# Attention stage of an encoder trunk: bulk loads move from SyncE's to GpSimd's DMA queue, and the scores' PSUM banks are laid out first

## The chip, the cores and the metric

The kernel runs on one core of a Trainium2 chip. Its time is in device microseconds (us). The engines that matter here are TensorE (PE), VectorE (DVE), ScalarE (ACT), GpSimd (POOL) and SyncE (SP). SP computes nothing; it issues DMAs, and in the kernel before it issues all of them.

## The reference, cut to what matters

Two groups of tokens (512 and 256, together 768) pass through two layers with shared weights. The change touches the first layer's windowed attention alone:

```python
qkv = h @ w_qkv                                   # h = rms_norm(x), 16 heads of 64, 4 kv heads
logits = einsum('bqgrd,bkgd->bgrqk', qb, kb) * scale + band_bias     # 128-query blocks, keys +-128
m = maximum(max(logits), sink_logit)
pexp = exp(logits - m)
denom = sum(pexp) + exp(sink_logit - m)           # a learned sink per head
probs = pexp / denom
out = einsum('bgrqk,bkgd->bqgrd', probs, vb)
x = x + out @ w_o
```

Behind it follow a squared-ReLU MLP with a gated embedding, then the second layer (a gated convolution in place of attention, and the same MLP and gate), and a last norm.

## The kernel before

**Tiling.** Channels lie on the 128 partitions, the 768 tokens on the free axis. Each float32 product is made of three float32r products (high times high, high times low, low times high); the halves of weights are made on the chip from a raw tile `wraw` (ACT writes `whi`, L657; DVE writes `wlo`, L661). `wraw` has three buffers, the pair `whi`/`wlo` two.

**The attention stage** (`mixer_attention`, L604) takes about the first 262 us of the span. It works group by group (four groups of four heads). `unit(c)` (L1202) fetches `w_q` for heads 2c and 2c+1, makes their product `mm` (L681), scales it into `qt` on DVE (L934, one piece of 512 and one of 256 tokens), splits it into `qh` (ACT) and `ql` (DVE), and then four DMAs from SBUF to SBUF stack high and low half of each head into a tile `q` (L979). Keys go the same way into `kk` (L963). For each of 24 blocks `attend` (L1062) runs: scores `S` on PE (L1087, L1088), reduction on DVE with the bias (L1094), exponential on ACT (L1104), scaling (L1117, L1119), transposes `pt` (L1130), their split `ph`/`pl` (L1139, L1140), products `O` (L1145) and the sum into `heads` (L1161). The sink's column of each logits tile `L` is written by 48 small copies on POOL (L1079), two heads each; `L` has five buffers.

**What sets the order.** In this stage nothing is ordered by program text. Every step is an `Op` with a cost, dependences, and for a DMA the time that its bytes take. `Plan.order` (L538) places them one by one: of the engine that can start first, the ready step with the longest remaining chain. Each engine then runs its steps in that order, and SP's DMAs are issued in that order too. All DMAs share one modelled pipe (L581), and SP may have eight in flight (`LANES`, L481, L572): the built program makes each DMA on SP wait for the landing of the eighth before it. A step of another engine may so change place whenever a cost changes.

**The DMAs of the stage** (L628 `dma`, L639 `fetched`): bulk loads from device memory (`w_q`, `w_k`, `w_v`, `w_o`, `proj`, `p` into `wraw`, and the residual `xa`, L1191); moves of queries and keys; the bias windows, eight DMAs of 96 KB for each group (L1055), read from a skewed table `skew` in device memory; and stores of the embedding's projection `pj`. All of these are on SP.

**PSUM.** The stage's pool gives eight banks by tag: `S` three, `PT` two, `O`, `mm0` and `mm1` one each. A tag gets its banks when the first tile of it is asked for, so in the kernel before `O` has bank 0, `mm0` bank 1, `mm1` bank 2, `PT` 3 and 4, `S` 5 to 7. Behind the stage a new pool of eight banks begins; its first product (L132) writes banks 0 and 1.

Of the kernel before, what the change touches and what calls it, by code (L numbers as in the profile page):

```python
# [10 lines left out]
F32 = mybir.dt.float32  # L11
# [6 lines left out]
P = 128  # L18
D = 1024
KB = D // P  # L20
# [9 lines left out]
BM, BS, BO, BT, BL = 1, 3, 1, 2, 5  # L30
# [20 lines left out]
def trunk_kernel(ctx: ExitStack, tc: tile.TileContext, a: dict, out: bass.AP):  # L51
    nc = tc.nc
    act, dve, pe = nc.scalar, nc.vector, nc.tensor
# [120 lines left out]
    class Norm:  # L174


        n = T
# [299 lines left out]
    class Plan:  # L477


        LATE = 6.0  # L480
        LANES = 8  # L481
        OWN = {"PE": 0.0, "ACT": 0.13, "DVE": 0.12, "POOL": 0.1, "SP": 0.0}
        OTHER = {"PE": 0.22, "ACT": 0.15, "DVE": 0.14, "POOL": 0.3, "SP": 0.1}

# [4 lines left out]
        def op(self, engine, cost, run, after=(), uses=(), behind=(), lands=None):  # L489
            flat = []  # L490
            for d in after:
                flat.extend(d if isinstance(d, (list, tuple)) else [d])
            o = Op(engine, cost, run, [d for d in flat if d is not None], list(behind), lands)
            for key in uses:
                assert key not in self.closed, key
                self.users.setdefault(key, []).append(o)
                if key in self.opened and self.opened[key] not in o.after:
                    o.behind.append(self.opened[key])
            self.ops.append(o)
            o.bonus = self.bonus if engine == "PE" else 0.0  # L500
            return o
# [9 lines left out]
        def first(self, box, engine, cost, run, after=(), uses=(), lands=None):  # L511

            def start():
                box.t = box.make()
                run()

            behind = [box.ahead.op] if box.ahead is not None and box.ahead.op is not None else []
            box.op = self.op(engine, cost, start, [box.free, *after], [box.key, *uses], behind, lands)
            self.opened[box.key] = box.op
            return box.op  # L520
# [17 lines left out]
        def order(self):  # L538
            after = {id(o): 0 for o in self.ops}
            nexts = {id(o): [] for o in self.ops}  # L540
            for o in self.ops:
                for d in o.after + o.behind:
                    nexts[id(d)].append(o)
                after[id(o)] = len(o.after) + len(o.behind)
            known, sorted_ = dict(after), [o for o in self.ops if after[id(o)] == 0]
            for o in sorted_:
                for n in nexts[id(o)]:
                    known[id(n)] -= 1
                    if known[id(n)] == 0:
                        sorted_.append(n)  # L550
            for o in reversed(sorted_):
                tail = o.tail + self.LATE if o.tail is not None else self.OTHER[o.engine]
                o.reach = o.cost + max((n.reach + (tail if o in n.after else 0.0) for n in nexts[id(o)]), default=0.0)
            free = {e: 0.0 for e in self.OWN}
            waiting = {e: [] for e in self.OWN}
            pipe, landings = 0.0, [0.0] * self.LANES

            def offer(o):
                o.ready = max(
                    [self.done(d, o.engine) for d in o.after] + [d.start for d in o.behind], default=0.0  # L560
                )
                waiting[o.engine].append(o)

            for o in self.ops:
                if after[id(o)] == 0:
                    offer(o)
            out = []
            while any(waiting.values()):
                best = None
                for e, os in waiting.items():  # L570
                    if os:
                        t = max(free[e], min(o.ready for o in os), landings[-self.LANES] if e == "SP" else 0.0)  # L572
                        o = max((o for o in os if o.ready <= t), key=lambda o: o.reach + o.bonus)
                        if best is None or t < best[0]:
                            best = t, o
                t, o = best
                waiting[o.engine].remove(o)
                o.start = t
                free[o.engine] = t + o.cost
                if o.tail is not None:  # L580
                    pipe = max(pipe, t + o.cost + 1.3) + o.tail  # L581
                    o.landed = pipe + 0.3
                    landings.append(o.landed)
                o.seq = len(out)
                out.append(o)
                for n in nexts[id(o)]:
                    after[id(n)] -= 1
                    if after[id(n)] == 0:
                        offer(n)
            assert len(out) == len(self.ops)  # L590
            return out
# [12 lines left out]
    def mixer_attention():  # L604
        nonlocal tmp
        s1 = ExitStack()
        psum = s1.enter_context(tc.tile_pool(name="psA", bufs=1, space=PSUM))
        ap = s1.enter_context(tc.tile_pool(name="attn", bufs=2))
        tmp = s1.enter_context(tc.tile_pool(name="tmpA", bufs=3))
        odd = s1.enter_context(tc.tile_pool(name="odd", bufs=2))  # L610

        KHI, KLO, QS = (0, 1, 4, 8), (2, 3, 5, 9), (6, 7, 14, 15, 10, 11, 12, 13)
        PB = {"mm0": 1, "mm1": 1, "S": BS, "O": BO, "PT": BT}
        W0 = SEQS[0]
# [13 lines left out]
        def dma(box, src, n, after=(), uses=(), queue="SP", rate=400e3):  # L628

            def run():  # L630
                d, s = src()
                (nc.sync if queue == "SP" else act).dma_start(d, s)

            lands = n / rate
            if box is not None and box.op is None:
                return first(box, queue, 0.46, run, after, uses, lands)
            return op(queue, 0.46, run, after, uses, lands=lands)

        def fetched(src):  # L639
            n = src.shape[1]  # L640
            raw = new("wraw", 3, lambda: wp.tile([P, CH], F32, name="wraw", bufs=3))
            raw.n = n
            raw.landed = [dma(raw, lambda: (raw.t[:, :n], src), P * 4 * n, uses=())]
            return raw

        def pair_tiles():
# [54 lines left out]
        def halves(w, xs, tags, col=0, fine=False):  # L701

            o, out = 0, []
            for tag, n in zip(tags, SEQS):
                ps = bank(tag)
                out.append((ps, o, n, product(ps, w, xs, o, n, col, fine)))
                o += n
            return out
# [479 lines left out]
        def load_part(ms):  # L1188
            for m in ms:
                xa[m] = place(m, "xa", F32)  # L1190
                xa[m].ready = [dma(xa[m], lambda m=m: (xa[m].t[:], a["x"][m]), 393216)]  # L1191

        def output_part(m, w, n, col=0):
            ops = []
# [5 lines left out]
                op("DVE", V(e), run, [last, xa[m].ready], [ps.key, xa[m].key])  # L1200

        def unit(c, tag):  # L1202
            queries(c, prepared(fetched(a["w_q"][c]), KB), ("mm0", "mm1"), tag)

        def second_keys():
            keys(1, halves(prepared(fetched(a["w_k"][1]), KB), xs, ("mm0", "mm1")), "t")

        def second_projected():
            ps = [pair(2 + p, "p1", F32R) for p in range(2)]
            part1 = []  # L1210
            for k in range(2):
                raw = fetched(a["p"][1, :, k, :])

                def high(k=k, raw=raw):
                    act.activation(ps[0].t[:, k, :], raw.t[:, :T], AF.Copy)

                def low(k=k, raw=raw):
                    dve.tensor_tensor(ps[1].t[:, k, :], raw.t[:, :T], ps[0].t[:, k, :].bitcast(F32), ALU.subtract)

                if k == 0:  # L1220
                    h = first(ps[0], "ACT", A(T), high, [raw.landed], [raw.key])
                    l = first(ps[1], "DVE", V(T), low, [h], [raw.key, ps[0].key])
                else:
                    h = op("ACT", A(T), high, [raw.landed, h], [raw.key, ps[0].key])
                    l = op("DVE", V(T), low, [h, l], [raw.key, ps[0].key, ps[1].key])
                b = Box()
                b.parts = lambda k=k: [p.t[:, k, :] for p in ps]
                b.ready, b.keys = [h, l], [p.key for p in ps]
                part1.append(b)
            w = prepared(fetched(a["proj"][1, 0]), 2)  # L1230
            for m in range(KB // 2):
                projected(1, m, w, part1, temp("n", "pjs"), ("mm0",), False)

# [16 lines left out]
        load_part(range(4))  # L1250
        group_of_heads(2)
        for j in range(2):
            w = prepared(fetched(a["w_o0"][j]), 4)
            for i in range(2):
                output_part(2 * j + i, w, 4, i * P)
        split_heads(2)
        load_part(range(4, KB))
        group_of_heads(3)
        for m in range(4, KB):
            output_part(m, prepared(fetched(a["w_o1"][m - 4]), 6), 6)  # L1260
        split_heads(3)
        with s1:
            with tc.manual_schedule(engines={ET.Activation, ET.PE, ET.DVE, ET.SP, ET.Pool}):
# [1193 lines left out]
```

## Time and profile before

| | us |
|---|---|
| median of three runs | 1643.17 |
| lowest, highest | 1642.59, 1643.72 |
| the profiled execution's own time | 1643.69 |
| span of its trace | 1641.9 |
| outside the span | 1.8 |

The page of the whole run reads: PE 1625.1 us busy (99% of the span), PE weight loads 1573.5 (96%), DVE 1389.6 (85%), ACT 920.6 (56%), POOL 12.3 (1%). The granted TensorE clock is at its full value in all 40 slices of the span. A busy PE in these views includes the overlap of pipelined matmuls, so a better measure of lost PE time is the idle time that the timeline puts in square brackets ahead of an instruction, with the event that ended it. The chain of work that ended last is 92% PE, 4% DVE and 2% DMA.

### The profile page before, as it was taken

How to read it: one execution, taken by the hardware profiler on the slowest of the kernel's cores; microseconds unless marked ns; L12 is line 12 of the kernel's file. 1: busy time of each engine (PE TensorE's matmuls, PEld its weight loads, DVE VectorE, ACT ScalarE, POOL GpSimd, SP SyncE). 2: the span in 40 equal slices, each digit the busy share in tenths (PEclk: the TensorE clock that was granted, in tenths of full speed). 3: DMA queues.
4: the chain of work that ended last, by engine and by line, in shares of the span. 5: the costliest groups of instructions: out<-in, count | busy, mean ns of one | idle time of the engine just before them, and what ended most of it. 6: DMA issues, size and time to landing. Idle time of an engine off the chain costs nothing.

```text
span 1641.9 us, 24136 instructions
## 1 busy us (share of the span) xinstructions
PE 1625.1 (99%) x9371; PEld 1573.5 (96%) x9371; DVE 1389.6 (85%) x2212; ACT 920.6 (56%) x1458; POOL 12.3 (1%) x60
## 2 busy tenths in 40 slices
PE   9999999999999999999999999999999999999998
PEld 7888889999999999999999999999999999999987
DVE  7578888999899989977878888768989989998686
ACT  7478885755555545545654344555555555654455
POOL 0000000000000000000000000000000000000000
PEclk9999999999999999999999999999999999999999
DMA  8745302212122212122311222211122121211322
GB/s 307 196 131 141 102 27 97 103 65 78 65 77 70 72 66 88 66 96 75 116 61 53 77 78 77 78 52 63 67 74 81 64 76 68 76 71 71 119 95 88
DMA packets 47822, 144.80 MB, mean 88 GB/s; under 512 B 6075, under 2 KB 9531, under 8 KB 47708
## 3 DMA queue, kind: packets, MB, share of 16 engines
q1 hardware_dynamic: 47708, 143.27, 25.7%
q8 instruction: 73, 1.20, 0.3%
q14 instruction: 41, 0.34, 0.1%
HBM read 123.85 MB, written 9.96 MB: 81 GB/s over the span
## 4 chain that ended last, share of the span: by engine, by line
PE 92%; DVE 4%; DMA 2%; ACT 1%; issue 1%; SPq 0%; DVEq 0%; ACTq 0%
PE a L465 33%; PE b L465 8%; PE mm L681 7%; PE mm L132 6%; PE p L1494 6%; PE d L465 5%; PE c L465 5%; PE gate L1828 4%; PE B L465 4%; PE C L465 4%; PE gate L132 3%; PE down L1828 2%; PE pt L1130 1%; PE O L1145 1%; PE S L1087 1%; PE S L1088 1%
## 5 line engine op out<-in xcount | busy, mean ns | idle before, releaser
L433 ACT ACTIVATE whi<-sum 128x1024 fp32r<-128x1024 f32 x66 | 70.2, 1063 | 253.6 <-PE a L465 251.8
L465 PE MATMUL a<-xs,whi 128*128 128x384 f32 x608 | 117.7, 334 | 0.0
L465 PEld LDWEIGHTS a<-xs,whi 128*128 128x128 f32 x608 | 106.4, 188 | 0.4 <-DVE t L2233 0.4
L465 PE MATMUL a<-t,zhi 128*128 128x384 f32 x528 | 106.6, 334 | 0.0
L465 PE MATMUL a<-t,whi 128*128 128x384 f32 x528 | 106.6, 334 | 0.0
L465 PE MATMUL b<-t,zhi 128*128 128x384 f32 x528 | 106.6, 334 | 0.0
L1650 DVE TENSOR_TENSOR x<-x,a 128x384 f32<-128x384 f32 x112 | 62.1, 554 | 51.5 <-PE a L465 51.5
L465 PE MATMUL a<-act,whi 128*128 128x384 f32 x448 | 95.6, 334 | 0.0
L465 PEld LDWEIGHTS a<-t,whi 128*128 128x128 f32 x528 | 92.9, 188 | 0.0
L465 PEld LDWEIGHTS b<-t,zhi 128*128 128x128 f32 x528 | 92.9, 188 | 0.0
L465 PEld LDWEIGHTS a<-t,zhi 128*128 128x128 f32 x528 | 92.9, 188 | 0.0
L433 ACT ACTIVATE zhi<-sum 128x1024 fp32r<-128x1024 f32 x66 | 69.8, 1057 | 40.8 <-DVE sum L409 26.1
L444 DVE TENSOR_TENSOR wlo<-wraw,whi 128x1024 fp32r<-128x1024 f32 x72 | 87.7, 1218 | 0.0
L433 ACT ACTIVATE whi<-wraw 128x1024 fp32r<-128x1024 f32 x72 | 75.7, 1052 | 20.1 <-issue 15.6
L444 DVE TENSOR_TENSOR zlo<-sum,zhi 128x1024 fp32r<-128x1024 f32 x66 | 80.4, 1218 | 0.7 <-ACT zhi L433 0.7
L681 PE MATMUL mm<-xs_mix,whi 128*128 128x512 f32 (+1 forms) x320 | 80.8, 339 | 0.0
L444 DVE TENSOR_TENSOR wlo<-sum,whi 128x1024 fp32r<-128x1024 f32 x66 | 80.4, 1219 | 0.0
L465 PEld LDWEIGHTS a<-act,whi 128*128 128x128 f32 x448 | 79.3, 188 | 0.0
L465 PE MATMUL a<-xs,wlo 128*128 128x384 f32 x304 | 64.9, 334 | 0.0
L465 PE MATMUL a<-t,wlo 128*128 128x384 f32 x264 | 60.9, 334 | 0.0
L465 PE MATMUL a<-t,zlo 128*128 128x384 f32 x264 | 60.9, 334 | 0.0
L465 PE MATMUL b<-t,zlo 128*128 128x384 f32 x264 | 60.9, 334 | 0.0
(391 smaller groups left out, 4477.3 us busy)
## 6 DMA issues: line engine op xcount, KB each, us to landing
wraw<-in_up SPq DMA_DIRECT2D x64, 512.0 KB, 3.4
wraw<-in_down SPq DMA_DIRECT2D x64, 512.0 KB, 3.4
wraw<-in_w_in SPq DMA_DIRECT2D x24, 512.0 KB, 3.5
wraw<-in_gate SPq DMA_DIRECT2D x16, 512.0 KB, 3.5
wraw<-in_w_q SPq DMA_DIRECT2D x8, 512.0 KB, 7.1
wraw<-in_w_out SPq DMA_DIRECT2D x8, 512.0 KB, 3.5
x_in<-in_x SPq DMA_DIRECT2D x8, 384.0 KB, 7.3
pj<-L SPq DMA_DIRECT2D x8, 384.0 KB, 5.7
```

Of the source, the lines that this page charges most:

```text
L132: pe.matmul(t, lhsT=w, rhs=x[:, o:e], start=first and i == 0 and j == 0, stop=last and i == n - 1 and j == 2)
L433: act.activation(hi[:], src, AF.Copy)
L444: dve.tensor_tensor(lo[:], src, hi[:].bitcast(F32), ALU.subtract)
L465: pe.matmul(ps, lhsT=a, rhs=b, start=start and i == 0, stop=i == len(terms) - 1, skip_group_check=True)
L681: pe.matmul(ps.t[:, :n], lhsT=a_, rhs=b_, start=k == 0 and j == 0, stop=k == len(xs) - 1 and j == 2,)
L1087: pe.matmul(S.t[:, :w], lhsT=q, rhs=khh_[g].t[:, kk], start=True, stop=False)
L1088: pe.matmul(S.t[:, :w], lhsT=q, rhs=kll_[g].t[:, kk], start=False, stop=True)
L1130: pe.transpose(pt.t[:, h * P : (h + 1) * P], lg[h // 2].t[:, h % 2, 1 + b * P : 1 + (b + 1) * P], ident[:],)
L1145: pe.matmul(O.t[:], lhsT=vb, rhs=part.t[:], start=b == 0 and i == 0, stop=b == nk - 1 and i == 1)
L1494: pe.matmul(ps[i][o], lhsT=wt[:, c], rhs=xs[f"x{h + 1}{1 + o}"][m][part], start=k == 0 and j == 0, stop=k == KB - 1 and j == 2,)
L1650: dve.tensor_tensor(t[:, o : o + H], t[:, o : o + H], f, op)
L1828: pe.matmul(ps.t[:, o : o + n], lhsT=a_, rhs=b_, start=begin and i == 0 and j == 0, stop=end and i == len(terms) - 1 and j == 2,)
```

## The change

It has three parts.

1. The bulk loads of the stage behind its first ones (`w_q` from the third on, the second `w_k`, the second layer's `p` and `proj`, all `w_o`, and the eight `xa`) are issued on POOL's queue. The start of the kernel (`proj`, `p`, `x`, `w_k`, two `w_q`, `w_v`) stays on SP, as do moves of queries and keys, the bias and the stores: of 367 DMA rows in SP's program 24 go to POOL's.
2. The planner counts 1.0 us of POOL for such an issue (0.46 on SP), has a pipe and a list of landings for each queue instead of one for all, and adds 1.0 us to a landing on POOL's. Its order of the whole stage is made anew with these numbers.
3. Ahead of everything else a tile of each of the tags `S`, `PT` and `O` is asked for, so `S` gets banks 0 to 2, `PT` 3 and 4, `O` 5, `mm0` 6 and `mm1` 7.

```diff
+        EXTRA = {"POOL": 1.0}
...
-            pipe, landings = 0.0, [0.0] * self.LANES
+            pipe, landings = {}, {e: [0.0] * self.LANES for e in self.OWN}
...
-                        t = max(free[e], min(o.ready for o in os), landings[-self.LANES] if e == "SP" else 0.0)
+                        t = max(free[e], min(o.ready for o in os), landings[e][-self.LANES] if e == "SP" else 0.0)
...
-                    pipe = max(pipe, t + o.cost + 1.3) + o.tail
-                    o.landed = pipe + 0.3
-                    landings.append(o.landed)
+                    pipe[o.engine] = max(pipe.get(o.engine, 0.0), t + o.cost + 1.3) + o.tail
+                    o.landed = pipe[o.engine] + 0.3 + self.EXTRA.get(o.engine, 0.0)
+                    landings[o.engine].append(o.landed)
...
+        for tag in ("S", "PT", "O"):
+            psum.tile([P, 512], F32, tag=tag, name="unused", bufs={"S": BS, "PT": BT, "O": BO}[tag])
...
-                (nc.sync if queue == "SP" else act).dma_start(d, s)
+                {"SP": nc.sync, "POOL": nc.gpsimd, "ACT": act}[queue].dma_start(d, s)
...
-        def fetched(src):
+        def fetched(src, queue="SP"):
...
-            raw.landed = [dma(raw, lambda: (raw.t[:, :n], src), P * 4 * n, uses=())]
+            raw.landed = [dma(raw, lambda: (raw.t[:, :n], src), P * 4 * n, queue=queue)]
...
-                xa[m].ready = [dma(xa[m], lambda m=m: (xa[m].t[:], a["x"][m]), 393216)]
+                xa[m].ready = [dma(xa[m], lambda m=m: (xa[m].t[:], a["x"][m]), 393216, queue="POOL")]
...
-            queries(c, prepared(fetched(a["w_q"][c]), KB), ("mm0", "mm1"), tag)
+            queries(c, prepared(fetched(a["w_q"][c], "POOL"), KB), ("mm0", "mm1"), tag)
...
-            w = prepared(fetched(a["w_o0"][j]), 4)
+            w = prepared(fetched(a["w_o0"][j], "POOL"), 4)
...
-            output_part(m, prepared(fetched(a["w_o1"][m - 4]), 6), 6)
+            output_part(m, prepared(fetched(a["w_o1"][m - 4], "POOL"), 6), 6)
```

Three places show what the new order does. The first is SP's queue in the middle of the stage, where the third and fourth groups' queries (`q`), the second keys and the bias are moved. Before:

```order
L632 DMA wraw<-in_w_o 128x1024
L632 DMA kk<-qh 64x768 x4
L632 DMA kk<-ql 64x768 x4
L632 DMA q<-qh 64x768 x2
L632 DMA wraw<-in_w_o 128x1024
L632 DMA q<-ql 64x768 x2
L632 DMA xa<-in_x 128x768 x2
L632 DMA bias<-skew 32x2x384 x8
L632 DMA q<-qh 64x768 x2
L632 DMA wraw<-in_w_o 128x768
L632 DMA q<-ql 64x768 x2
```

and now:

```order
L635 DMA kk<-qh 64x768 x4
L635 DMA kk<-ql 64x768 x4
L635 DMA q<-qh 64x768 x2
L635 DMA q<-ql 64x768 x2
L635 DMA bias<-skew 32x2x384 x8
L635 DMA q<-qh 64x768 x2
L635 DMA q<-ql 64x768 x2
```

The two loads of `w_o` that stood between a query's high and low halves, and the two of `xa` ahead of the bias, are gone from the queue; the eight bias DMAs still stand ahead of the next queries.

The second place is POOL's queue over the same stretch and a little beyond, where before only the sink copies stood (48 in a row):

```order
L1083 COPY L<-nsink 128x2 x10
L635 DMA wraw<-in_w_o 128x1024
L635 DMA xa<-in_x 128x768 x2
L1083 COPY L<-nsink 128x2 x4
L635 DMA wraw<-in_w_o 128x768
L1083 COPY L<-nsink 128x2 x4
L635 DMA wraw<-in_w_o 128x768
```

The loads now stand among the copies, which go on in the order of the blocks that need them.

The third place is PE, between the projection of heads 10 and 11 (`mm`, for the query tile that is read at the end) and the first scores that read that tile (`q_2004` before, `q_2007` now). The last rows before:

```order
L681 MATMUL mm_1939<-xs_mix0_372,wlo_1812 128x512
L681 MATMUL mm_2053<-xs_mix0_181,whi_1811 128x256
L681 MATMUL mm_2053<-xs_mix0_193,whi_1811 128x256
L681 MATMUL mm_2053<-xs_mix0_181,wlo_1812 128x256
L681 MATMUL mm_2053<-xs_mix0_230,whi_1811 128x256
L681 MATMUL mm_2053<-xs_mix0_257,whi_1811 128x256
L681 MATMUL mm_2053<-xs_mix0_230,wlo_1812 128x256
L681 MATMUL mm_2053<-xs_mix0_261,whi_1811 128x256
L681 MATMUL mm_2053<-xs_mix0_282,whi_1811 128x256
L681 MATMUL mm_2053<-xs_mix0_261,wlo_1812 128x256
L1087 MATMUL S_2066<-kk_1538,q_2004 128x256
```

and now:

```order
L1149 MATMUL O_2041<-pl_2043,vv_105 128x512
L685 MATMUL mm_1942<-xs_mix0_375,whi_1814 128x512
L685 MATMUL mm_1942<-xs_mix0_407,whi_1814 128x512
L685 MATMUL mm_1942<-xs_mix0_375,wlo_1815 128x512
L1091 MATMUL S_2056<-kk_1541,q_2007 128x256
```

The nine matmuls on 256 tokens have gone from ahead of the scores. Otherwise the same 36 matmuls stand between the last one of that projection and these scores: 21 `mm` on 512 tokens, 2 `S` on 256, 5 `O` and 8 transposes.

More of the change, by code (lines that the diff above doesn't have):

```diff
@@ L631, in run @@
                 d, s = src()
-                (nc.sync if queue == "SP" else act).dma_start(d, s)
+                {"SP": nc.sync, "POOL": nc.gpsimd, "ACT": act}[queue].dma_start(d, s)
             lands = n / rate
+            cost = 1.0 if queue == "POOL" else 0.46
             if box is not None and box.op is None:
-                return first(box, queue, 0.46, run, after, uses, lands)
-            return op(queue, 0.46, run, after, uses, lands=lands)
-        def fetched(src):
+                return first(box, queue, cost, run, after, uses, lands)
+            return op(queue, cost, run, after, uses, lands=lands)
+        def fetched(src, queue="SP"):
             n = src.shape[1]
@@ L1202, in unit @@
         def unit(c, tag):
-            queries(c, prepared(fetched(a["w_q"][c]), KB), ("mm0", "mm1"), tag)
+            queries(c, prepared(fetched(a["w_q"][c], "POOL"), KB), ("mm0", "mm1"), tag)
         def second_keys():
-            keys(1, halves(prepared(fetched(a["w_k"][1]), KB), xs, ("mm0", "mm1")), "t")
+            keys(1, halves(prepared(fetched(a["w_k"][1], "POOL"), KB), xs, ("mm0", "mm1")), "t")
         def second_projected():
@@ L1211, in second_projected @@
             for k in range(2):
-                raw = fetched(a["p"][1, :, k, :])
+                raw = fetched(a["p"][1, :, k, :], "POOL")
                 def high(k=k, raw=raw):
@@ L1229, in second_projected @@
                 part1.append(b)
-            w = prepared(fetched(a["proj"][1, 0]), 2)
+            w = prepared(fetched(a["proj"][1, 0], "POOL"), 2)
             for m in range(KB // 2):
```

## The prediction, made before the change was run

> **What bounds the kernel now.** I read the page first, then the windows, then the waits, and last the timelines at the places that the waits name. The page's chain of work that ended last:
>
> ```profile
> PE 92%; DVE 4%; DMA 2%; ACT 1%; issue 1%; SPq 0%; DVEq 0%; ACTq 0%
> ```
>
> PE sets the end nearly everywhere, so only a stretch in which PE waits can give time back. The windows (busy us of PE, PEld, DVE, ACT, POOL; clock; DMA share; GB/s) show where such stretches lie:
>
> ```profile
> 100.00:125.00 25.00, 24.84 (x152) 21.27 (x151) 24.01 (x73) 24.76 (x65) 1.85 (x10) 1.00 0.58 181
> 150.00:175.00 25.00, 20.94 (x122) 17.90 (x121) 18.03 (x52) 15.26 (x41) 2.24 (x6) 1.00 0.59 141
> 300.00:325.00 25.00, 25.00 (x147) 25.00 (x146) 21.76 (x32) 16.50 (x22) 0.00 (x0) 1.00 0.15 55
> ```
>
> Behind the attention stage PE is full (300 to 325 us). Inside it most windows are nearly full too; the one from 150 to 175 us lacks 4 us, on PE, DVE and ACT alike, so all three wait there for something else. The waits over 100 to 250 us name it, and PE's timeline shows each place (start, length, what ran; in brackets the idle time before it and what ended it):
>
> ```profile
> PE S L1087 <- DMA q<-ql: 4.8, 3, 2.7
> ```
>
> ```profile
> 155.35 0.35 PE L1087 MATMUL S<-kk,q 128*128 128x256 f32 x1 [1.34 <-DMA q<-ql]
> ...
> 167.53 0.36 PE L1087 MATMUL S<-kk,q 128*128 128x256 f32 x1 [2.71 <-DMA q<-ql]
> ...
> 207.04 0.39 PE L1087 MATMUL S<-kk,q 128*128 128x256 f32 x1 [0.75 <-DMA q<-ql]
> ...
> 262.33 0.94 PE L132 MATMUL mm<-aos,whi 128*128 128x384 f32 x4 [0.60 <-DVE xa L1198]
> ```
>
> Three times scores wait for the low half of their queries, 4.8 us in all; and the first product behind the stage waits 0.60 us until DVE has emptied a bank. That is all that this change can win by removing waits. SP's queue tells why the queries are late:
>
> ```profile
> 146.61 1.10 SPq L632 DMA_DIRECT2D q<-qh  x2
> 147.81 0.53 SPq L632 DMA_DIRECT2D wraw<-in_w_o  x1
> 148.44 1.10 SPq L632 DMA_DIRECT2D q<-ql  x2
> 149.63 1.09 SPq L632 DMA_DIRECT2D xa<-in_x  x2
> 150.82 8.95 SPq L632 DMA_DIRECT2D bias<-skew  x8
> 159.87 1.11 SPq L632 DMA_DIRECT2D q<-qh  x2
> 161.07 0.54 SPq L632 DMA_DIRECT2D wraw<-in_w_o  x1
> 161.71 1.10 SPq L632 DMA_DIRECT2D q<-ql  x2
> ```
>
> A load of `w_o` stands between the halves each time, and the eight bias issues take 8.95 us, because SP waits for the landing of the eighth DMA before: of the waits of SP's queue from 146 to 162 us,
>
> ```profile
> SPq L632 <- DMA xa<-in_x: 2.8, 2, 1.7
> SPq L632 <- DMA wraw<-in_w_o: 1.9, 1, 1.9
> ```
>
> What a query's move costs without and with a load ahead of it, from issue to landing (median us), is in the DMA view of 92 to 98.5 us, where nothing else is in flight, and of 140 to 165 us:
>
> ```profile
> q<-ql SPq DMA_DIRECT2D x4, 192.0 KB, 4.0
> ```
>
> ```profile
> q<-ql SPq DMA_DIRECT2D x4, 192.0 KB, 6.2
> ```
>
> **The change part by part.** *The first wait (1.34 us).* PE's rows up to these scores (`q_1840`) are the same in number and kind before and now. DVE and ACT made this query's halves here, and the next one's 12 us later:
>
> ```profile
> 147.02 0.95 DVE L716 TENSOR_TENSOR ql<-qt,qh 128x768 fp32r<-128x768 f32 x1
> ...
> 156.45 0.42 DVE L934 SCALAR_TENSOR_TENSOR qt<-mm,rstd_mix 128x256 f32<-128x256 f32 x1
> ...
> 158.90 0.95 DVE L716 TENSOR_TENSOR ql<-qt,qh 128x768 fp32r<-128x768 f32 x1
> ```
>
> The low half is ready at 147.97; issued at once and landing in 4.0 us, it is there at 152.0, and PE came to the scores at 155.35 - 1.34 = 154.0. I take the whole 1.34; the other end is 0, if `w_o` on its own queue slows the move as much as one ahead of it does.
>
> *The second wait (2.71 us).* PE's work between the projection and these scores shrinks by nine matmuls on 256 tokens. Their price, and that of the 36 that stay, from the chain in order of time:
>
> ```profile
> 174.11 0.36 PE mm L681 x3
> ...
> 175.59 0.68 PE mm L681 x3
> 176.26 0.23 PE O L1145
> 176.50 0.87 PE pt L1130 x8
> ```
>
> Three matmuls on 256 tokens take 0.36, so 0.12 each; three on 512 take 0.68, 0.23 each; eight transposes 0.87. The nine are 1.1 us, which are not lost but run later. What stays is 21 x 0.23 + 2 x 0.12 + 5 x 0.23 + 0.87 = 7.1 us. The projection is done when its last `qt` starts, 156.45, so PE reaches the scores at 163.5. The low half is ready at 158.90 + 0.95 = 159.85; before, it was issued at 161.71. With `w_o` and `xa` off SP neither of the two waits of SP above stands ahead of it, and at 159.9 + 4.0 it lands at 163.9. I leave 0.5 us of waiting and take 2.2 saved; the ends are 0 and 2.71.
>
> *The third wait (0.75 us).* `w_o` is gone from between the halves, and counted with the same prices PE has 9.2 us of work ahead of the first scores of heads 14 and 15 instead of 8.0. All 0.75 are taken (ends 0 and 0.75).
>
> *The bank (0.60 us).* Banks 0 and 1, which L132 writes first, are now two of the scores' banks, last read several us earlier, and no longer `O` and `mm0`. `mm0` and `mm1` (now 6 and 7) are asked for only two products later. I take 0.60; the ends are 0 and 0.60.
>
> *What it costs.* Sooner scores in the first group: there PE's work between the projection of heads 2 and 3 and their first scores falls from 8.9 to 7.5 us (12 value products on 256 tokens no longer stand there). In exchange a load of `p` is gone from between the high halves on SP:
>
> ```profile
> 67.05 0.53 SPq L632 DMA_DIRECT2D wraw<-in_p  x1
> ```
>
> That load's issue of 0.53 and its share of the DMA engines go, 1.4 of cover go; I put 0.3 for it, between 0 and 1.4. Then POOL: no load is issued there before, so its price is bounded by the nearest rows: 0.53 (SP's issue) from below; from above, two sink copies that took 1.50, 1.13 more than the 0.37 of the row shown next:
>
> ```profile
> 158.40 1.50 POOL L1079 COPY L<-nsink 128x2 f32<-128x2 f32 x2 [6.32 <-PE pt L1130]
> ```
>
> so 0.5 to 1.7 us an issue. Queued behind a load are the sink copies, for which DVE's reduction waits. Nine of the 24 loads come ahead of the sixth copy, fifteen stand among the others. What hides them is that a copy is made when its `L` comes free, mostly some us ahead of the reduction; early it is not so:
>
> ```profile
> 97.64 0.37 POOL L1079 COPY L<-nsink 128x2 f32<-128x2 f32 x2 [57.50 <-PE pt L1130]
> ```
>
> ```profile
> 97.84 0.61 DVE L1094 CUSTOM_DVE_ANT_0 L<-S,bias,nsink 128x384 f32<-128x384 f32 x1
> ```
>
> At 97.84 the reduction follows the first copy at once. I put 0.5 us for one such late copy, nearest to the lower row; the ends are 0 and 17 (15 x 1.13). That the loads themselves land later costs nothing at first: before, ACT waited 0.3 us in all for a `w_q`,
>
> ```profile
> ACT whi L657 <- DMA wraw<-in_w_q: 0.3, 1, 0.3
> ```
>
> as each is fetched while earlier products run; without that cover each later landing would hold ACT's queue.
>
> *The sum:* 1.34 + 2.2 + 0.75 + 0.60 = 4.9 won, 0.3 + 0.5 lost, 4.1 in all. From the profiled execution's 1643.69 that leaves 1639.6. That execution lies 0.52 above the median of the runs, so the forecast is **1639.1**.
>
> **The rivals.** *Same bytes, same engines.* The loads are only put in another queue, and share the DMA engines with the queries at the same moments (their share is 0.59 over 150 to 175 us). If a move beside `w_o` takes the 6.2 us that it took behind it, the three waits stay, and only the bank's 0.60 is won, with 0.8 of costs: 1643.4. For it speaks that the load still starts about when the query's halves are ready; against it that FIFO order put all 512 KB ahead of 192 KB, and that sharing puts at most as much. The Trainium skill has this as a rule ("DMA: Bandwidth & Descriptors", section "Issuing engines are not separate DMA queues"): DMAs of all issuing engines run on the same 16 DMA engines and interleave, and a second issuer saves only the time of issuing. By that rule this rival is the case; the trace so far shows order within one queue, none between two.
>
> *POOL's queue holds DVE* (the slower side). A load on POOL waits in order for its buffer and then takes POOL; the copies behind it come late, the reductions on DVE with them, and DVE has no room (24.01 of 25 us busy from 100 to 125). With half of 15 x 1.13 on the path, 8.5 us in place of my 0.5, it ends at 1647.1. It eats the gain when each of the fifteen costs the path 0.31 us (4.6 / 15), and makes the kernel slower by 0.2% from 0.53 on. For it speaks the row with 1.50; against it, the row at 97.64, whose copies took 0.37 beside a DVE at work. The skill ("SBUF — State Buffer", section "SBUF: two separate sides") names a cause that would bring it about: GpSimd cannot write a DMA's descriptors while certain VectorE instructions hold a port that both share. No run here has yet shown such a DMA.
>
> That the planner's new order loses PE time elsewhere is part of both; PE's rows are the same kinds in the same number.
>
> **How the numbers follow.** Forecast 0.52, same bytes 0.25, POOL's queue 0.23. A measurement of this kernel can tell about 0.2%, 3.3 us, from no change: faster means below 1639.9, slower above 1646.5. The forecast's own range is 1637 to 1641, of which about three quarters lie below 1639.9 (0.40) and the rest within 0.2% (0.12); the second case lies within (0.24, and 0.01 above); the third is slower (0.23). The range goes from 1637 (both costs nothing, and all 2.71 saved: 1637.8, with a little for a better order elsewhere) to 1648, into the third case.
>
> **What would show it.** In the profile after, the waits of `S` L1087 for `q<-ql` should fall from 4.8 us to under 1, the eight bias issues from 8.95 us to about 4, `q<-ql` to near 4.0 us to landing, and L132 should start with no wait for `xa`. Waits of `L` L1094 for POOL, or of `whi` L657 for DMAs of POOL's queue, would speak for the slower rival; waits for `q<-ql` as before for the other. The forecast is wrong if PE's loss over 100 to 262 us does not shrink.

## The result: 0.58% slower, and the profile after

| | before | after |
|---|---|---|
| median, us | 1643.83 (6 runs) | 1653.71 (6 runs) |
| lowest, highest | 1642.59, 1644.41 | 1649.83, 1655.70 |
| profiled execution: own time, span | 1643.69, 1641.9 | 1655.32, 1653.5 |
| start of the first product behind the attention stage (L132) | 262.33 | 273.13 |
| from there to the end of the span | 1379.6 | 1380.4 |

The ratio of the times is 1.0058, 95% interval 1.0047 to 1.0069. The last two rows say where to look: 10.8 of the 11.6 us that the span grew lie inside the attention stage. Lines of that stage have moved down by four in the new kernel (scores L1091, values L1018, reduction L1098, `xa` L1202, the split of `p` L1219 and L1222).

Three views of the profile after. The first is the chain of work that ended last; DMA had 2% of it before:

```profile
PE 88%; DVE 5%; DMA 4%; ACT 1%; issue 1%; SPq 0%; DVEq 0%; POOL 0%; ACTq 0%; POOLq 0%
```

The second is PE's timeline at the places of the stage from 50 us on where it stood still for half a microsecond or more (start, length; in brackets the idle time and what ended it):

```profile
55.92 0.48 PE L1018 MATMUL vp<-wvh,xs_mix 128*128 128x256 f32 x1 [3.29 <-DVE vv L1036]
...
80.24 0.55 PE L1091 MATMUL S<-kk,q 128*128 128x256 f32 x1 [3.07 <-DMA q<-ql]
...
164.73 0.36 PE L1091 MATMUL S<-kk,q 128*128 128x256 f32 x1 [1.34 <-DMA q<-ql]
...
175.05 0.36 PE L1091 MATMUL S<-kk,q 128*128 128x256 f32 x1 [1.92 <-DMA q<-ql]
...
214.47 0.35 PE L1091 MATMUL S<-kk,q 128*128 128x256 f32 x1 [1.77 <-DMA q<-ql]
...
273.13 0.94 PE L132 MATMUL mm<-aos,whi 128*128 128x384 f32 x4 [0.60 <-DVE xa L1202]
```

The first two are new. The first wait of before (1.34) and the bank's 0.60 are unchanged to the hundredth, 2.71 became 1.92, and 0.75 became 1.77. The third view is windows of 4 us around the two new gaps and the one at 175 us (busy PE, PEld, DVE, ACT, POOL; granted clock; DMA share; GB/s):

```profile
52.00:56.00 4.00, 0.71 (x4) 0.27 (x2) 1.35 (x2) 1.21 (x2) 0.12 (x1) 1.00 1.04 223
56.00:60.00 4.00, 4.00 (x18) 3.71 (x19) 0.00 (x0) 0.00 (x0) 0.42 (x1) 0.57 1.06 230
...
80.00:84.00 4.00, 3.76 (x14) 3.38 (x15) 1.74 (x5) 1.21 (x4) 0.00 (x0) 0.58 0.39 131
...
176.00:180.00 4.00, 4.00 (x18) 3.71 (x17) 2.25 (x8) 1.91 (x6) 0.00 (x0) 0.63 0.02 6
```

Behind each of these gaps PE worked for some 3.5 us at a granted clock of about half. Worked out as busy time times the missing clock, that cost 1.7, 1.6 and 1.5 us more. Before, the granted clock was 1.00 in the windows behind its longest gap, 2.71 us.

So the account of the stage is: 5.0 us at 52 us (3.29 and the clock), 4.7 at 77, 0.7 at 173 (1.92 and 1.5 against 2.71), and 1.0 at 212. That is 11.4, against 10.8 by which the stage became longer.

**How the gap at 52 us comes about** is told by ACT's timeline, before and after:

```profile
50.76 0.48 ACT L1029 ACTIVATE vv<-vp,rc 128x256 fp32r<-128x256 f32 x1 [4.24 <-PE vp L1016]
61.35 0.84 ACT L1215 ACTIVATE p<-wraw 128x768 fp32r<-128x768 f32 x1 [10.12 <-DMA wraw<-in_p]
```

```profile
53.64 0.84 ACT L1219 ACTIVATE p<-wraw 128x768 fp32r<-128x768 f32 x1 [7.29 <-DMA wraw<-in_p]
54.39 0.46 ACT L1033 ACTIVATE vv<-vp,rc 128x256 fp32r<-128x256 f32 x1
```

Before, ACT waited longer for the second layer's `p` (10.12 us), but the value copy `vv` stood ahead of it, so nothing was held up by that. Now the same split of `p` stands ahead of `vv`; the in-order engine holds `vv` until the load has landed, and PE's next value product waits for the bank that `vv` and DVE's half of it must empty. The DMA view of 43 to 51 us has the load and its neighbours (KB each, median us from issue to landing):

```profile
kk<-qh SPq DMA_DIRECT2D x4, 192.0 KB, 9.0
...
wraw<-in_p POOLq DMA_DIRECT2D x1, 384.0 KB, 7.9
```

The planner's own sum for that load on a POOL pipe that is free is 1.0 (issue) + 1.3 + 393216/400000 + 0.3 + 1.0 = 4.6 us. It took 7.9, beside moves of keys that the plan has on another pipe with a full rate of its own. At 77 us it is the same with a move: on SP's free pipe the plan's sum for two moves behind each other is 0.46 + 1.3 + 2 x 196608/215000 + 0.3 = 3.9 us, and in the DMA view of 72 to 79 us

```profile
wraw<-in_proj POOLq DMA_DIRECT2D x1, 512.0 KB, 6.8
...
q<-ql SPq DMA_DIRECT2D x2, 192.0 KB, 6.8
```

### The profile page after: what moved, and what is told of

Its sections match the earlier page's. It is cut to its first block, busy times and chain, and to the rows that moved or that the text cites. A ratio compares the mean times of both kernels' runs of the same rounds, so it can differ in the third digit from the quotient of the medians.

```text
span 1653.5 us, 24160 instructions
## 1 busy us (share of the span) xinstructions
PE 1629.2 (99%) x9371; PEld 1576.8 (95%) x9371; DVE 1390.1 (84%) x2212; ACT 920.6 (56%) x1458; POOL 24.4 (1%) x84
## 4 chain that ended last, share of the span: by engine, by line
PE 88%; DVE 5%; DMA 4%; ACT 1%; issue 1%; SPq 0%; DVEq 0%; POOL 0%; ACTq 0%; POOLq 0%
PE a L465 33%; PE b L465 8%; PE mm L132 6%; PE p L1498 6%; PE mm L685 6%; PE d L465 5%; PE c L465 5%; PE B L465 4%; PE C L465 4%; PE gate L1832 3%; PE gate L132 2%; PE down L1832 2%; DMA q<-ql 1%; PE pt L1134 1%; PE O L1149 1%
```

## The experiments

Two theories were set against each other. *Order:* the loss comes from the new order of steps on in-order engines, planned with landings that are too early, since each queue has a pipe of its own. *Queue:* loads on POOL's queue cost by themselves.

### 1. The queue alone (e1), the order alone (e2), the banks alone (e3), one pipe (e4)

e1 keeps the planner and banks of before (`cost` is 0.46 for all), so PE, ACT and DVE have the order of before, row for row (the edit against the kernel before, cut):

```diff
+                {"SP": nc.sync, "POOL": nc.gpsimd, "ACT": act}[queue].dma_start(d, s)
...
+            return op("SP" if queue == "POOL" else queue, cost, run, after, uses, lands=lands)
```

> The 24 bulk loads are issued on POOL's queue, but the planner still counts them on SP with one common pipe, so PE, ACT and DVE run their steps in the order of the kernel before; the banks are as before. Order theory (the loss comes from the steps' new order, which rests on landings that the planner puts too early because each queue has a pipe of its own): 1641 to 1645 us, the two new PE stalls at 52 and 77 us (3.3 and 3.2 us) are gone. Queue theory (loads on POOL's queue cost by themselves, through shared DMA engines, POOL's time or later landings): at least 6 of the 10 us stay, 1649 to 1655.

Measured: 1645.84 us, ratio 1.0013 (1.0004 to 1.0022), 0.8 us beyond the range of the order theory; the stage ends at 265.1 us. Both new gaps are gone, and most of the loss with them, but not all of it. Two other waits for queries nearly cancel (a new one of 0.76 us at 74 us, and the second wait down from 2.71 to 0.98). What is left of the loss lies at the third wait, 0.75 us before, and in 1.6 us of low clock behind it; on PE's timeline:

```profile
208.56 0.36 PE L1089 MATMUL S<-kk,q 128*128 128x256 f32 x1 [3.10 <-DMA q<-ql]
```

The DMA views of 198 to 209 us, of before and of e1, tell why:

```profile
q<-qh SPq DMA_DIRECT2D x2, 192.0 KB, 2.9
wraw<-in_w_o SPq DMA_DIRECT2D x1, 384.0 KB
q<-ql SPq DMA_DIRECT2D x2, 192.0 KB, 5.2
```

```profile
xa<-in_x POOLq DMA_DIRECT2D x1, 384.0 KB, 5.5
q<-qh SPq DMA_DIRECT2D x2, 192.0 KB, 6.6
q<-ql SPq DMA_DIRECT2D x2, 192.0 KB, 7.8
wraw<-in_w_o POOLq DMA_DIRECT2D x1, 384.0 KB, 7.5
```

In one queue the high halves were issued ahead of `w_o` and landed in 2.9 us, as if it were not there. From two queues everything in flight shares the DMA engines, and all of it lands late: 6.6 us for the high halves, 7.8 instead of 5.2 for the low ones, and 5.5 for the last load of `xa`, where the last two took 3.5 before (DMA view of 197 to 198 us). Sharing does not explain all of it: the low halves were issued 1.1 us sooner than before (200.62 against 201.74), with about the same bytes moved (2.0 MB in either view), and still landed 1.5 us later. The rest stays open. The Trainium skill has the rule ("DMA: Bandwidth & Descriptors", section "Issuing engines are not separate DMA queues"): DMAs of all issuing engines run on the same 16 engines and interleave. The runs agree: a second queue is no second set of engines. They add that a move can lose by it.

e2 is the reverse: order and banks of the changed kernel, all loads on SP.

```diff
-                {"SP": nc.sync, "POOL": nc.gpsimd, "ACT": act}[queue].dma_start(d, s)
+                {"SP": nc.sync, "POOL": nc.sync, "ACT": act}[queue].dma_start(d, s)
```

> The changed kernel's order and banks, but its 24 bulk loads are issued on SP's queue at the place that the order gives them. Order theory: the value copy on ACT still stands behind the split of the second layer's in_p, so the PE stall at 52 us stays at 2 us or more and the time is 1649 to 1658 us. Queue theory: near the kernel before, 1642 to 1646.

Measured: 1657.69 us, ratio 1.0088 (1.0074 to 1.0102), slower than the change as a whole. PE stands for 4.62 us at 52 us, and loses the clock again:

```profile
57.42 0.50 PE L1018 MATMUL vp<-wvh,xs_mix 128*128 128x256 f32 x1 [4.62 <-DVE vv L1036]
```

The order brings the loss without POOL's queue. In this order the second queue even helps.

e3 adds only the two lines of the banks to the kernel before.

```diff
+        for tag in ("S", "PT", "O"):
+            psum.tile([P, 512], F32, tag=tag, name="unused", bufs={"S": BS, "PT": BT, "O": BO}[tag])
```

> The kernel before with the scores' banks first in the pool; every engine's order as before. If the bank that L132 waits for was the one that the output's sum still read, 0.60 us of idle time at 262 us go and the time is 1642.6. If the wait is for the whole pool, or for another bank that the same sum reads, the 0.60 us stay, and the time is that of the kernel before within 0.5 us. The order theory needs the second; no theory has this part cost anything.

Measured: 1643.35 us, ratio 1.0001 (0.9992 to 1.0009), and in PE's timeline

```profile
261.36 0.94 PE L132 MATMUL mm<-aos,whi 128*128 128x384 f32 x4 [0.60 <-DVE xa L1200]
```

The products write banks 0 and 1, which are now the scores', and still wait for the last sum on DVE, which reads another bank. It isn't for data either, since the product reads `aos` and `whi` and not `xa`. So the wait isn't that of the bank. That it hangs on the whole pool being given back is likely, but was not tried.

e4 is the changed kernel with one pipe in the planner.

```diff
-            pipe, landings = {}, {e: [0.0] * self.LANES for e in self.OWN}
+            pipe, landings = 0.0, {e: [0.0] * self.LANES for e in self.OWN}
...
+                    pipe = max(pipe, t + o.cost + 1.3) + o.tail
+                    o.landed = pipe + 0.3 + self.EXTRA.get(o.engine, 0.0)
```

> The changed kernel, but the planner has one common pipe for all DMAs again; its issue cost of 1.0 us on POOL, its added landing of 1.0 us and the banks stay. Its order is then almost that of the kernel before on PE. Order theory: 1641 to 1646 us, no stall of 3 us at 52 or 77. Queue theory: 1649 to 1655.

Measured: 1647.31 us, ratio 1.0023 (1.0014 to 1.0032): 1.3 us beyond what the order theory gave, far from what the queue theory gave. The pipe alone so accounts for 6.4 of the 9.9 us by which the changed kernel was slower. The gap at 52 us is gone; four waits for queries are left, two of 1.4 us at 159 and 170 and two longer ones, each with the low clock behind it:

```profile
75.34 0.36 PE L1091 MATMUL S<-kk,q 128*128 128x256 f32 x1 [2.21 <-DMA q<-ql]
...
211.54 0.36 PE L1091 MATMUL S<-kk,q 128*128 128x256 f32 x1 [2.65 <-DMA q<-ql]
```

### 2. Later landings in the plan (e5 to e7)

If the plan's landings are too early, adding to them must help, with the queues as they are. e5:

```diff
-        EXTRA = {"POOL": 1.0}
+        EXTRA = {"POOL": 6.0}
```

> The changed kernel, but the planner adds 6 us instead of 1 to a landing on POOL's queue. PE's order stays that of the changed kernel between projections and scores; on ACT the split of the second layer's in_p falls from ahead of the second value copy to behind it. Order theory: only the stall at 52 us goes, 3.4 us, and with it the 1.7 us in which the granted clock was 0.66 behind it: 1647 to 1650 us, the stalls at 77, 163, 173 and 212 us stay. If the low clock has another cause than the idle time, it stays and the time is 1650 to 1651. Queue theory: 1652 or more, since no load moves to another queue.

Measured: 1649.43 us, ratio 1.0038 (1.0025 to 1.0050). The gap at 52 us is gone, and the clock behind it is whole; of the two windows, the second is the one that had 0.57 in the changed kernel:

```profile
52.00:56.00 4.00, 4.00 (x26) 3.48 (x25) 0.48 (x1) 0.48 (x1) 0.00 (x0) 1.00 1.02 205
56.00:60.00 4.00, 4.00 (x28) 3.66 (x27) 0.96 (x1) 0.85 (x1) 0.54 (x1) 1.00 1.06 222
```

The stage became 3.6 us shorter than the changed kernel's, not 5.0, because the wait of 1.92 us grew to 3.03, with twice as long a low clock behind it:

```profile
170.55 0.55 PE L1091 MATMUL S<-kk,q 128*128 128x256 f32 x1 [3.03 <-DMA q<-ql]
```

e6 corrects both queues by about what the traces show:

```diff
-        EXTRA = {"POOL": 1.0}
+        EXTRA = {"POOL": 4.0, "SP": 3.0}
```

> The changed kernel, but the planner adds 4 us to a landing on POOL's queue and 3 us to one on SP's, so that it plans with about the 6 to 8 us that loads and moves took beside each other. PE's work between a projection and its first scores grows from 7.5 to 10.2 us for heads 2 and 3, from 7.1 to 10.1 for heads 10 and 11, and from 9.2 to 10.9 for the last. Order theory: the stalls at 52, 77, 173 and 212 us shrink to under 1 us each, and the time is 1640 to 1645. Queue theory: 1649 or more. A third possibility is that the later scores leave DVE and ACT idle and PE loses as much elsewhere: 1646 to 1650.

Measured: 1638.75 us, ratio 0.9970 (0.9958 to 0.9981): faster than both kernels, 15 us below the changed one, and 1.2 us below what the order theory gave. Two waits for queries are left on PE's timeline:

```profile
155.76 0.36 PE L1091 MATMUL S<-kk,q 128*128 128x256 f32 x1 [1.15 <-DMA q<-ql]
...
166.72 0.35 PE L1091 MATMUL S<-kk,q 128*128 128x256 f32 x1 [0.59 <-DMA q<-ql]
```

e7 has the order of e6 with all loads issued on SP (the edit of e2 on top of that of e6).

> The order of the kernel that counts both queues' landings 3 to 4 us later, but all its loads are issued on SP's queue, in that order. It tells what the queue is worth once the order leaves time for the landings. Order theory: the queue is worth little by then, within 2 us of the same order with POOL's queue. If two queues really help (as with the changed kernel's own order, which was 4 us slower on SP alone): 3 to 6 us slower. If POOL's queue costs by itself: faster.

Measured: 1640.02 us, ratio 0.9975 (0.9964 to 0.9985). The intervals of e6 and e7 overlap widely. Once the order leaves room for the landings, the queue is worth nothing that can be told here.

### 3. The kernel before with later landings (e8, e9, e11), and two queues on one pipe (e10)

With that, the change isn't needed for the gain. e8, e9 and e11 are the kernel before, all DMAs on SP, with 1.5, 3 and 6 us added to every landing in the plan; for e8:

```diff
-                    o.landed = pipe + 0.3
+                    o.landed = pipe + 1.8
```

> The kernel before, all DMAs on SP and one common pipe, but its planner adds 1.5 us to every landing. PE's work ahead of the first scores grows from 8.2 to 9.4 us for heads 10 and 11 and from 8.0 to 11.2 for the last, with ql ahead of w_o at heads 10 and 11. Order theory: the waits for queries (4.8 us before) fall to 1 to 2 us, and the kernel beats both, 1639 to 1642. If the later scores cost DVE and ACT as much: 1642 to 1646.

Measured: 1639.36 us, ratio 0.9972 (0.9960 to 0.9983).

> The kernel before with 3 us instead of 1.5 added to every landing in its planner, all DMAs on SP. PE's work ahead of the first scores grows to 12.0 us (heads 2 and 3), 11.5 (8 and 9), 10.8 (10 and 11) and 16.3 (the last). With 1.5 us only one wait for queries is left, 0.9 us. If more room is simply better, that one goes too and the time is 1638 to 1639. If room has a price, because DVE and ACT get their scores later and PE then waits for them, 1640 to 1644; the waits of S would be for mn or for a bank.

Measured: 1637.08 us, ratio 0.9953 (0.9941 to 0.9966), the fastest of all and 0.9 us below the range expected. No score waits for a query any more. The window of 150 to 175 us, in which PE had 20.94 us of work before and 21.79 after the change, is full:

```profile
150.00:175.00 25.00, 25.00 (x152) 22.04 (x151) 19.77 (x58) 17.86 (x44) 1.78 (x6) 1.00 0.61 138
```

> The kernel before with 6 us added to every landing in its planner, all DMAs on SP; PE's work ahead of the first scores grows to 15.2, 14.7, 14.3 and 21.1 us, more than any landing took. With 3 us no wait for queries was left, so nothing is to be won. Order theory: room beyond the landing is worth nothing, the time is that with 3 us, 1637 to 1638. If room has a price, in scores that come late for DVE and ACT, 1639 to 1645.

Measured: 1645.88 us, ratio 1.0012 (1.0003 to 1.0021), above both ranges. The number alone would say that room has a price of 9 us, but the stage doesn't show it: it ends at 256.9 us, 1.3 later than in e9 and 5.4 earlier than before. From there to the end it took 1386.9 us, where every other run had 1379.0 to 1380.8. The loss lies in the second layer, some 1275 us later, where PE waits twice for a weight that ACT makes, at 1532 us (PE's timeline) and for 1.68 us at 1579, each time 0.53 us more for its low half, and loses 1.7 us to the clock behind the first; that is 6.7 of some 7.4 us:

```profile
1532.66 0.73 PE L1828 MATMUL down<-act,whi 128*128 128x512 f32 x2 [2.22 <-ACT whi L1816]
```

Rows of that part stand in another order than before, which they do in e8 and e9 too, without a loss. What ties them to the stage's plan was not tried. So 6 us were too late a plan by 1.3 us in the stage itself; the rest stays open.

e10 is the changed kernel with one pipe, 0.55 us for an issue on POOL, and 1.5 us added to landings on both queues.

```diff
+        EXTRA = {"POOL": 1.5, "SP": 1.5}
...
+            cost = 0.55 if queue == "POOL" else 0.46
```

> Two queues as in the changed kernel and its banks, but the planner has one common pipe, counts 0.55 us for an issue on POOL as measured, and adds 1.5 us to every landing. Order theory: as the kernel before with the same 1.5 us, 1638 to 1641, whichever queue the loads are in. If two queues let loads crowd out the moves even then, 1642 to 1646, with waits of S for ql of 3 us or more in all.

Measured: 1639.20 us, ratio 0.9968 (0.9956 to 0.9980), as e8 with one queue.

| run | order planned with | loads on | stage ends | ratio |
|---|---|---|---|---|
| before | one pipe | SP | 262.3 | 1 |
| e1 | one pipe | POOL | 265.1 | 1.0013 |
| e4 | one pipe, POOL's own costs | POOL | 268.1 | 1.0023 |
| after | a pipe per queue | POOL | 273.1 | 1.0058 |
| e2 | a pipe per queue | SP | 274.8 | 1.0088 |
| e5 | a pipe per queue, POOL's landings +6 us | POOL | 269.6 | 1.0038 |
| e6 | a pipe per queue, landings +4, +3 us | POOL | 258.2 | 0.9970 |
| e7 | the same | SP | 259.0 | 0.9975 |
| e8, e10 | one pipe, +1.5 us | SP, POOL | 258.4, 257.9 | 0.9972, 0.9968 |
| e9 | one pipe, +3 us | SP | 255.6 | 0.9953 |
| e11 | one pipe, +6 us | SP | 256.9 | 1.0012 (lost behind the stage) |

Read down, the end of the stage follows the order. With the order held, the queue moves the ratio by +0.0013 (before and e1), by -0.0030 (e2 and after), and not measurably (e7 and e6). e8 and e10 came out alike, but PE's rows in them stand in different orders, so this pair says nothing of the queue by itself.

## Why the prediction was wrong, step by step

The forecast was 1639.1, the range 1637 to 1648; it came out slower, at 1653.71. The view that carried it was read rightly: PE is the bound, and the waits for queries were what could be won. e9 won them (its stage is 6.7 us shorter, more than the 4.8 of the waits; where the rest came from stays open). The change did not: of the 4.9 us to be won it won 0.8, at the second wait, and lost that and more again there and at the third. By size, though, the steps that failed are the price of the new order, put at nothing for ACT's queue (it cost 5.0 us at 52 us) and at 0.3 for the cover lost at heads 2 and 3 (4.7 us).

- *First wait, 1.34 saved:* nothing was. The cover came out as computed: from the ready low half to PE's arrival 6.0 us, before and after. The step that failed is "issued at once and landing in 4.0 us". The 4.0 came from a stretch with nothing else in flight; beside `w_o` on POOL this move took 7.2 us (median), against 6.9 behind it in one queue. The price was taken from the wrong row: 6.2 stood beside it. That the wait is the same to the hundredth is chance.
- *Second wait, 2.2 saved:* of 2.71 us 1.92 stayed, and PE then lost 1.5 to the clock. The same mistake, smaller: PE's work ahead (7.3 us) came out as computed, and the move took 5.3 us beside the `w_o` that POOL issued at 169.22. What came off SP's queue went onto the same engines at the same moment.
- *Third wait, 0.75 saved:* it grew to 1.77. e1 shows the mechanism, with the cover of before unchanged. The sentence that sharing "puts at most as much" ahead of the move as FIFO does not save the move: it took 7.8 us instead of 5.2, and landed 1.5 us later although it was issued sooner. That the high halves, which were ahead of the load, now share with it is part of that; what the rest is stays open.
- *The bank, 0.60 saved:* it stayed to the hundredth, in the change and alone (e3). The banks were right; that the wait is the bank's was wrong.
- *Sooner scores, 0.3, ends 0 to 1.4:* cover lost was counted as if the move still landed in time. It landed in 6.8 us beside `proj`, cover was 7.5 from the projection's last matmul, with `qt` and the split of its halves still to come: 3.07 us, and 1.6 for the clock. This term was off fifteenfold.
- *POOL's issues, 0.5:* about right, and harmless. They took mostly 0.53 to 0.55 us each, and no instruction of DVE waited for POOL. Nearly alone, a load from POOL's queue landed fast, as in the DMA view of 76 to 84 us:

```profile
wraw<-in_w_q POOLq DMA_DIRECT2D x1, 512.0 KB, 3.7
```

- *"Each later landing would hold ACT's queue":* this named the mechanism of the largest loss, but put its price at nothing, from `w_q` alone. It was `in_p`, and what mattered was not the load's landing but what the new order had put behind it. "That the planner's new order loses PE time elsewhere is part of both" passed over it; that PE's rows are the same in kind says nothing of what ACT and DVE hold back.
- *The rivals:* "same bytes, same engines" had the mechanism of the queue right, and of the two numbers that it gave, its move of 6.2 us was too short at the first wait (7.2) and the third (8.3, DMA view of 204 to 212 us), and its sum of 1643.4 left the order out; e1, the queue by itself, measured 1645.84. "POOL's queue holds DVE" fell: no wait of `L` L1098 for POOL. A rival in which a wrong plan costs PE time by itself was missing.

Of the signs named beforehand, the eight bias issues did get shorter, from 8.95 us to 5.51 on SP's queue; `whi` waited 1.1 us for a `w_q`, against 0.3 before; the waits of `S` for `q<-ql` over 100 to 262 us did not shrink, and that was the stated condition under which the forecast is wrong:

```profile
PE S L1091 <- DMA q<-ql: 5.0, 3, 1.9
```

## What to carry to other kernels

Where a static order is planned, the model of the DMAs is part of the kernel: a second queue that shares the DMA engines must share the model's pipe, and a landing planned too early holds work that was ready on in-order engines, and here 1.5 to 3 us added to every landing won 0.3 to 0.5%. Price a move from a row in which the same neighbours are in flight, not from a quiet stretch. Before a transfer is put in another queue, ask what FIFO order did for it: in e1 the small moves ahead of a load lost that protection.

## What the hardware showed unexpectedly

Short idle times cost PE twice. Behind most gaps of 1.8 to 4.6 us PE ran for 3.4 us (once, in e5, for 6.8) at half its clock, at a price of 1.5 to 1.7 us, half of a 3 us gap again. In PE's timeline of the changed kernel, behind the first gap, two matmuls on 512 tokens take 0.85 us from start to start of the next, where three took 0.68 in the prediction's rows:

```profile
57.91 1.05 PE L685 MATMUL mm<-xs_mix,whi 128*128 128x512 f32 x2
58.76 0.63 PE L685 MATMUL mm<-xs_mix,wlo 128*128 128x512 f32 x1
```

The length of a gap does not decide by itself: one of 1.79 us in e3 was followed by a window at 0.57, one of 1.77 us in the changed kernel by windows at 1.00, and so was the 2.71 us of the kernel before:

```profile
156.00:160.00 4.00, 4.00 (x18) 3.40 (x17) 3.20 (x8) 3.88 (x9) 0.75 (x2) 0.57 0.76 155
```

```profile
216.00:220.00 4.00, 4.00 (x29) 3.67 (x27) 3.62 (x11) 2.34 (x9) 0.37 (x2) 1.00 0.25 100
```

(the first of e3, the second of the changed kernel). What decides is where the gap falls, which the record of the granted clock in the traces shows. In the changed kernel the low stretches begin at 56.06, 79.95 and 175.52 us and last 3.41 us each, and from the first to the others it is 7 and 35 times 3.413 us. In every run that has low stretches they stand on such a grid, and the record's first entry, 4.9 to 7.6 us into the span, lies on it too. Continued through the span (from the first entry in runs without a low stretch), this grid cuts each gap into parts. PE's idle time within one stretch of the grid then sorts all thirteen runs:

| idle time within one stretch of 3.41 us | clock in the next stretch |
|---|---|
| 3.30 (e2) down to 1.92 (after) and 1.79 (e3), 13 stretches | half |
| 1.60 (e5), 1.50 (e2) and 1.43 (before, from its gap of 2.71) and less | full |

So in these runs the bound lies between 1.60 and 1.79 us, near half a stretch. One case is outside the rule: in e5 a stretch at half clock with 0.74 us idle was followed by a second one at half. And a low clock costs nothing where PE would have waited anyway: e3 had one behind its gap at 155 us, and the second wait, 2.71 us before, is down to 0.24 there. Since the grid does not start with the kernel, the same gap can cost the clock in one execution and not in the next. The executions of the changed kernel, from 1649.83 us at a mean clock of 0.997 to 1655.70 at 0.994, fit that.

The Trainium skill ("TensorE: Matmul & The Clock Gate", section "Part 1: The HAM clock gate") describes a clock that halves after about 3.4 us of idle time, seen in windows that run freely. The half rate and the grid agree; the idle time that sufficed here is shorter, 1.79 us within a window.
